# Table products and weight splits from GpSimd to VectorE, key copies to ScalarE, readout tables behind the chunk contributions

## The chip, the cores and the metric

One core of a Trainium2 chip runs the whole kernel. The metric is device microseconds of one execution, median of several runs.

## The reference

One layer for 256 latent tokens and 256 context tokens of width 1024. What the change touches lies in the first sub-layer:

```python
h  = modulate(rmsnorm(x, g1),   sh1,  sc1)      # latents
hc = modulate(rmsnorm(ctx, g1), sh1c, sc1c)     # context
proj, proj_c = h @ w_in, hc @ w_in[:, :COL_Q]   # S5 input | K | V | Q | gates
lbar = exp(lam * step); bbar = ((lbar - 1) / lam) * b
for direction in (forward, backward):           # 32 groups, 64 complex states each
    h_c = scan(lbar, u_c @ bbar)                # context, its last state starts the latents
    hs  = scan(lbar, u @ bbar, h0=h_c[end])
    y  += real(hs @ c)
q, k = rope(rmsnorm(q)), rope(rmsnorm(k))       # k of the context without rope
o = softmax(q k_all / 8) v_all
merged = gate0 * (glu(y) @ w_ssm_out) + gate1 * (o @ w_attn_out)
x_mix = x + g1 * (merged @ w_out)
```

Behind it come a second norm, a router that takes the top 4 of 32 experts, clamped SwiGLU experts of width 1024 with 12 MB of weights each, and a last norm.

## The kernel before, in words

SBUF is used as 24 pages of 1 MB (`pg(i)`), which are given out by hand. `release(p)` frees a page and issues on SP's queue the next 1 MB of a fixed list of weights: eight gate blocks of w_in, then w_glu, w_ssm_out, w_attn_out, w_out, then the experts one after the other. SP's loads stand in program order, so a load waits for its page and holds the ones behind it. The order on the other engines up to the gates is set by a scheduler that goes by its own idea of durations and of what is urgent; from `strict["on"]` on, TensorE's order is that of the program, and VectorE's, ScalarE's and GpSimd's still the scheduler's.

Products that need more than the plain pass are made from two halves of each operand: `split(src, hi, lo, eng)` rounds src into hi on ScalarE (line 62) and subtracts on `eng` (line 63). `mm3` is the three products of the halves.

The front part runs in this order:

1. Norm sums, the modulation of the first sub-layer (`mod0_mm`, `mod0_rows`), and VectorE's chain for lbar and the powers E of it, up to 47 us.
2. The input projection of the S5 branch (`u_mm`, `u_proj`). Its second half needs `wuh, wul`, split from w_in in four pieces (line 643), of which GpSimd subtracted two.
3. The S5 tables. `v_tables(qt)` for four quarters of the groups makes bbar times powers (real part VR, imaginary VI; six operations of 128x1024 in each); VI of quarters 0 and 1 lay on GpSimd. `v_transposes` turns them on TensorE. `scan_multipliers` makes the scan's constants LS (lines 521 to 529, 128x32 each). `w_tables(qt)` makes the readout tables WR, WI, c times powers, six operations of 128x1024 for each quarter, all on GpSimd (lines 608 to 613), three quarters behind `mod_tile` and the fourth behind the U copies.
4. `kv_proj`, the transposes of u into A (copies on line 704) and U (line 717).
5. The chunk contributions: `chunk_in(i)` and `chunk_T(i)` for eight pairs of group quads, copied half by VectorE (line 747), half by ScalarE (line 748); two `q_proj` lie between.
6. Rotary and norm of q and k (`rope_norm`, lines 789 to 819). A copy of each normed key block lay on GpSimd (line 822).
7. Sixteen steps u: `gate_mm(u // 2, u % 2)` multiplies the gate block whose weights `gate_split` has split (32 pieces of 128x512, subtracted on GpSimd) and asks for the next block's split; eight of the steps make `k_kernel(u)`, taps R of the S5 kernel from the W tables (last piece added on line 970); VectorE runs `scan_up` and 31 `scan_steps` (lines 855 to 858). From step 9 on attention runs beside it. R goes through DRAM (`Rd`) and comes back as Kt; `readout` uses Kt, the states and WR, WI.
8. GLU, the two branch projections, w_out, router, experts.

Of the kernel before, what the change touches and what calls it, by code (L numbers as in the profile page):

```python
# [15 lines left out]
AF = mybir.ActivationFunctionType  # L16
# [17 lines left out]
def hybrid_block(ctx: ExitStack, tc: tile.TileContext, a: dict, out: bass.AP):  # L34
    nc = tc.nc
    V, S, G, T = nc.vector, nc.scalar, nc.gpsimd, nc.tensor
# [10 lines left out]
    def renew(i, kind="f"):  # L47
        if i not in pages or epoch[i] != kind:
            pages[i], epoch[i] = pool.tile([128, PW], F32, name=f"pg{i}", tag=f"pg{i}"), kind
# [4 lines left out]
    def pg(i, o=0, n=PW):  # L54
        return pages[i][:, o:o + n]
# [5 lines left out]
    def split(src, hi, lo, eng):  # L61
        S.activation(hi.bitcast(F32R), src, AF.Copy)  # L62
        eng.tensor_sub(lo.bitcast(F32R), src, hi)  # L63
# [25 lines left out]
    def load(dst, src):  # L89
        return tc.keep_in_program_order(SP.dma_start(dst, src))  # L90
# [30 lines left out]
    def load_cols(src, c0, n, page, k0, nk):  # L121
        t = pg(page, 0, nk * n).rearrange("p (k f) -> p k f", k=nk)
        load(t, src[128 * k0:128 * (k0 + nk), c0:c0 + n].rearrange("(k p) f -> p k f", p=128))
        return t


    stream, loaded, where = [], {}, {}
# [23 lines left out]
    def release(*ps):  # L151
        for p_ in ps:
            renew(p_)
            j = state["next"]
            state["next"] = j + 1
            if j < len(stream):
                key, src = stream[j]
                k, f = src.shape[1], src.shape[2]
                t = pg(p_, 0, k * f).rearrange("p (k f) -> p k f", k=k)
                if j == len(stream) - 1:  # L160
                    for k in (0, 4):
                        load(t[:, k:k + 4], src[:, k:k + 4])
                else:
                    load(t, src)
                loaded[key], where[key] = t, p_
            elif j == len(stream):
                state["fg"] = p_
                fg_row = pg(p_, 1024, 1024)[0:1]
                load(fg_row, a["final_norm_g"][None, :])
                G.partition_broadcast(pg(p_, 0, 1024), fg_row)  # L170
# [39 lines left out]
    wu = [load_cols(w_in, 0, 512, 22, 0, 4)]  # L210
# [42 lines left out]
    def bank(hold=None):  # L253
        while True:
            i = rot["free"][rot["i"] % len(rot["free"])]
            rot["i"] += 1
            if i not in held.values():
                break
        if hold:
            held[hold] = i  # L260
        return named_bank(i)
# [288 lines left out]
    def v_part(qt, r):  # L550
        return pg(vpage[qt], 1024 * r, 1024).rearrange("p (g t k) -> p g t k", g=8, t=8)

    def v_tables(qt):
        gs = slice(8 * qt, 8 * qt + 8)
        td = pg(7, 0, 1024).rearrange("p (g t k) -> p g t k", g=8, t=8)

        def bc(r):
            return BB[:, r, gs].unsqueeze(2).to_broadcast([128, 8, 8, 16])

        def lc(r):  # L560
            return LV[:, r, :, gs].rearrange("p t g -> p g t").unsqueeze(3).to_broadcast([128, 8, 8, 16])

        VR, VI = v_part(qt, 0), v_part(qt, 1)
        V.tensor_mul(VR, bc(0), lc(0))
        V.tensor_mul(td, bc(1), lc(1))
        V.tensor_sub(VR, VR, td)
        E2 = V
        if qt < 2:
            E2, td = G, pg(20, 0, 1024).rearrange("p (g t k) -> p g t k", g=8, t=8)
        E2.tensor_mul(VI, bc(0), lc(1))  # L570
        E2.tensor_mul(td, bc(1), lc(0))
        E2.tensor_add(VI, VI, td)  # L572

    def v_transposes(qt):
        for g2 in range(4):
# [18 lines left out]
    WR, WI = [], []  # L594

    def w_tables(qt):
        gs = slice(8 * qt, 8 * qt + 8)
        td = pg(20, 1024 * (qt % 2), 1024).rearrange("p (g j k) -> p g j k", g=8, j=8)
        for r, tab in ((0, WR), (1, WI)):
            tab.append(pg((18, 19, 11, 12)[qt], 1024 * r, 1024).rearrange("p (g j k) -> p g j k", g=8, j=8))  # L600

        def cc(r):
            return CT[:, r, gs].unsqueeze(2).to_broadcast([128, 8, 8, 16])

        def lw(r):
            return LW[:, r, :, gs].rearrange("p t g -> p g t").unsqueeze(3).to_broadcast([128, 8, 8, 16])

        G.tensor_mul(WR[qt], cc(0), lw(0))
        G.tensor_mul(td, cc(1), lw(1))
        G.tensor_add(WR[qt], WR[qt], td)  # L610
        G.tensor_mul(WI[qt], cc(1), lw(0))
        G.tensor_mul(td, cc(0), lw(1))
        G.tensor_sub(WI[qt], WI[qt], td)

# [23 lines left out]
    renew(11, "r")  # L640
    wuh, wul = [pg(p_).rearrange("p (k f) -> p k f", k=4) for p_ in (12, 11)]
    for k in range(4):
        split(wu[1][:, k], wuh[:, k], wul[:, k], V if k % 2 else G)
    last = mod0_rows(1)
    del held["m", 0], held["m", 1]
    with tc.issue_after(last.ins):
# [17 lines left out]
    mod_tile()  # L664
    renew(11)
    renew(12)
    for qt in range(3):
        w_tables(qt)
    v_transposes(1)
    v_tables(3)  # L670
    v_transposes(2)
# [45 lines left out]
            V.tensor_copy(U[:, 4 * g4:4 * g4 + 4, :, h], b.rearrange("p (g q c) -> p g q c", g=4, q=4))  # L717

    mod_tile()
    w_tables(3)  # L720
    split(wq[1], wqh[1], wql[1], V)
    mod_load(16)

# [15 lines left out]
    def chunk_T(i, vo):  # L739
        b = bank()  # L740
        for j in range(2):
            for r in range(2):
                ttrans(b[:, 128 * (2 * r + j):128 * (2 * r + j) + 128],
                            vo[:, 256 * j + 128 * r:256 * j + 128 * r + 128], ident)
        for h in range(2):
            bv = b.rearrange("p (r g h c) -> p h c r g", r=2, g=4, h=2)[:, h]
            V.tensor_copy(vv[h][0:64, :, :, 4 * i:4 * i + 4], bv[0:64])
            S.activation(vv[h][64:128, :, :, 4 * i:4 * i + 4], bv[64:128, ::-1], AF.Copy)

    prev = None  # L750
    for i in range(8):
# [6 lines left out]
        if i in (2, 4):  # L758
            q_proj(i // 2 - 1)
    chunk_T(7, prev)  # L760
    release(20)
    renew(4)

    wgh, wgl_ = [pg(p_).rearrange("p (j k f) -> p j k f", j=2, k=8) for p_ in (13, 10)]

    def gate_split(i, j):
        for k in range(0, 8, GK):
            sl = slice(k, k + GK)
            split(loaded["gate", i][:, sl, 128 * j:128 * j + 128], wgh[:, j, sl], wgl_[:, j, sl], G)


    cosq, sinq = sm([128, 2, 64], "cosq"), sm([128, 2, 64], "sinq")
# [8 lines left out]
    kn = pg(5, 0, 1024).rearrange("p (t h d f) -> p t h d f", t=4, h=2, d=2)  # L781
# [31 lines left out]
    for tt in range(4):  # L813
        kvw = kv_ps[tt // 2].rearrange("p (t h f) -> p t h f", t=2, h=4)[:, tt % 2, 0:2]
        r_k = rsn[:, 16 + 2 * tt:18 + 2 * tt]
        d0 = kn[:, tt, :, 0]
        if tt < 2:
            V.tensor_mul(d0, kvw, kg_row.unsqueeze(1).to_broadcast([128, 2, 64]))
            V.tensor_mul(d0, d0, r_k.unsqueeze(2).to_broadcast([128, 2, 64]))
        else:  # L820
            rope_norm(d0, kvw, cosk[:, tt - 2], sink[:, tt - 2], r_k, 2, d0)
        G.tensor_copy(kn[:, tt, :, 1], d0)


    qs = pg(22).rearrange("p (t h r f) -> p t h r f", r=2, t=2, h=8)
# [323 lines left out]
    for u in range(16):  # L1149
# [5 lines left out]
        i = u // 2 + 1  # L1155
# [116 lines left out]
    gate, posp, ex_, mrep = [sm(sh3, n) for n in ("gate", "posp", "ex_", "mrep")]  # L1272
# [450 lines left out]
```

## Time and profile before

| what | value |
|---|---|
| median of 3 runs | 1323.57 us (1322.31 to 1325.38) |
| the profiled execution | 1321.38 us, span 1319.7 us |
| TensorE busy | 1170.8 us (89%), mean granted clock 0.966 |
| VectorE busy | 439.7 us (33%) |
| ScalarE busy | 196.5 us (15%) |
| GpSimd busy | 158.1 us (12%), 115 instructions |
| read from HBM | 459.89 MB, 350 GB/s over the span |
| chain that ended last | TensorE 49%, DMA 37%, VectorE 10% |

The shares are means over stages that differ: VectorE's and GpSimd's work lies nearly all in the first 330 us. A timeline row gives the start, the duration, the engine, the line of the program, the operation, the tiles written and read with their shapes, the count, and in brackets how long the engine stood idle before it and what ended that. A row with a count above 1 is a stretch from the first start to the last end.

### The profile page before, as it was taken

The page shows a single profiled execution, that of the slowest core. Times are in us where ns is not written, and L with a number is a line of the kernel's source. Part 1 is how long each engine was busy: PE and PEld are TensorE (multiplying, and loading weights), DVE is VectorE, ACT ScalarE, POOL GpSimd, SP SyncE. Part 2 cuts the span into 40 slices and gives each one's busy share as a digit, 9 for nine tenths or more (in the row PEclk, how much of TensorE's full clock was granted, in tenths as well). Part 3 has the DMA queues.
Part 4 walks back from the last instruction along what each step waited for, and adds up shares of the span by engine and source line. Part 5 has one row for each costly group of instructions (what it writes and reads, how often), then busy time and mean ns, then how long its engine had stood idle before and what let it go on. Part 6 is the DMA issues. An engine that isn't in the chain of part 4 may idle for free.

```text
span 1319.7 us, 16264 instructions
## 1 busy us (share of the span) xinstructions
PE 1170.8 (89%) x6711; PEld 541.5 (41%) x6712; DVE 439.7 (33%) x929; ACT 196.5 (15%) x368; POOL 158.1 (12%) x115
## 2 busy tenths in 40 slices
PE   4563998689999999999999989999898989899986
PEld 2363666578843333333332323323232323233224
DVE  5999389757331121111221111121111111111111
ACT  3231343654110000000000000000000000000001
POOL 1479563412000000000000000000000000000000
PEclk9876899889999999999999999999999999999998
DMA  9810567777989999999999999999999999999996
GB/s 277 279 33 33 191 233 240 116 219 276 352 337 416 416 417 416 416 418 417 418 418 417 418 417 416 417 416 417 417 418 417 417 417 417 417 417 415 416 392 205
DMA packets 123105, 462.57 MB, mean 351 GB/s; under 512 B 20669, under 2 KB 46953, under 8 KB 88210
## 3 DMA queue, kind: packets, MB, share of 16 engines
q1 hardware_dynamic: 122562, 460.90, 89.7%
q8 instruction: 55, 0.90, 0.3%
q0 software_dynamic: 416, 0.56, 0.1%
q14 instruction: 24, 0.20, 0.0%
q10 hardware_dynamic: 48, 0.01, 0.0%
HBM read 459.89 MB, written 1.54 MB: 350 GB/s over the span
## 4 chain that ended last, share of the span: by engine, by line
PE 49%; DMA 37%; DVE 10%; issue 2%; SPq 1%; ACT 1%; POOL 0%; DVEq 0%; ACTq 0%; POOLq 0%
PE bk L83 46%; DMA pg<-in_w_gate_up_dram 28%; DMA pg<-in_w_down_dram 7%; PE bk L86 3%; DMA pg<-Rd 1%; DVE pg L63 1%; DVE pg L858 1%; SPq L90 1%; DVE LS L528 1%; DVE LS L855 1%; DVE pg L522 0%; DVE LS L523 0%; DVE pg L848 0%; DVE pg L380 0%; DVE LS L529 0%
## 5 line engine op out<-in xcount | busy, mean ns | idle before, releaser
L83 PE MATMUL bk<-pg,pg 128*64 128x512 f32 (+6 forms) x5344 | 995.6, 476 | 65.6 <-DMA pg<-in_w_down_dram 28.3
L83 PEld LDWEIGHTS bk<-pg,pg 128*64 128x64 f32 (+3 forms) x5344 | 448.3, 154 | 552.4 <-issue 351.8
L86 PE MATMUL bk<-ident,pg 128*128 128x128 f32 x480 | 83.0, 301 | 57.3 <-DVE pg L572 21.0
L1460 DVE TENSOR_SCALAR pg<-bk 128x512 f32<-128x512 f32 x32 | 22.1, 692 | 290.7 <-PE bk L83 290.7
L1371 DVE TENSOR_TENSOR pg<-bk,shT 128x512 f32<-128x512 f32 x32 | 22.1, 692 | 266.4 <-PE bk L83 266.4
L86 PEld LDWEIGHTS bk<-ident,pg 128*128 128x128 f32 x480 | 56.6, 150 | 123.0 <-issue 48.1
L1577 POOL DMA_DIRECT2D pg<-g2d x2 | 1.3, 642 | 882.2 <-PE bk L83 882.2
L1493 DVE TENSOR_TENSOR pg<-bk,pg 128x512 f32<-128x512 f32 x30 | 20.8, 692 | 188.8 <-PE bk L83 188.8
L1472 ACT ACTIVATE pg<-bk 128x256 f32<-128x256 f32 x32 | 12.3, 383 | 395.4 <-PE bk L86 395.4
L83 PE MATMUL bk<-pg 64*128 64x512 f32 (+1 forms) x368 | 70.5, 486 | 0.0
L1477 ACT ACTIVATE pg<-bk 128x512 f32<-128x512 f32 x32 | 19.1, 596 | 257.4 <-PE bk L86 257.4
L63 POOL TENSOR_TENSOR pg<-pg,pg 128x512 fp32r<-128x512 f32 x34 | 47.5, 1412 | 43.8 <-ACT pg L62 36.8
L62 ACT ACTIVATE pg<-pg 128x512 fp32r<-128x512 f32 (+3 forms) x63 | 43.7, 721 | 56.8 <-PE bk L83 35.8
L1461 ACT ACTIVATE pg<-pg 128x512 f32<-128x512 f32 x32 | 20.1, 630 | 187.0 <-DVE pg L1460 186.9
L83 PEld LDWEIGHTS bk<-pg 64*128 64x128 f32 (+1 forms) x368 | 20.0, 162 | 50.4 <-issue 50.4
L63 DVE TENSOR_TENSOR pg<-pg,pg 128x512 fp32r<-128x512 f32 (+3 forms) x29 | 33.7, 1176 | 3.3 <-ACT pg L62 2.9
L83 PE MATMUL bk<-pg,selB 128*64 128x512 bf16 (+1 forms) x196 | 34.4, 388 | 0.0
L83 PE MATMUL bk<-pg,scond 128*32 128x256 f32 (+1 forms) x256 | 29.0, 525 | 0.0
L1462 DVE TENSOR_SCALAR pg<-bk 128x512 f32<-128x512 f32 x32 | 22.1, 692 | 5.3 <-PE bk L83 5.3
L1463 DVE TENSOR_TENSOR pg<-pg 128x512 f32<-128x512 f32 x32 | 21.8, 683 | 2.1 <-ACT pg L1461 2.0
L1464 DVE SCALAR_TENSOR_TENSOR pg<-pg 128x512 f32<-128x512 f32 x32 | 22.1, 692 | 1.1
L1468 DVE TENSOR_SCALAR pg<-iot,posp,gate 128x128 f32<-128x128 f32 x64 | 18.9, 340 | 0.0
(301 smaller groups left out, 539.1 us busy)
## 6 DMA issues: line engine op xcount, KB each, us to landing
pg<-in_w_gate_up_dram SPq DMA_DIRECT2D x256, 1024.0 KB, 20.0
pg<-in_w_down_dram SPq DMA_DIRECT2D x127, 1024.0 KB, 20.0
pg<-in_w_mod_dram SPq DMA_DIRECT2D x16, 1024.0 KB, 5.4
pg<-in_w_in_dram SPq DMA_DIRECT2D x13, 1024.0 KB, 9.0
pg<-in_w_mod_dram SPq DMA_DIRECT2D x16, 512.0 KB, 9.1
pg<-in_w_out_dram SPq DMA_DIRECT2D x4, 1024.0 KB, 11.8
pg<-Rd SPq DMA_DIRECT2D x16, 128.0 KB, 8.5
pg<-in_w_ssm_out_dram SPq DMA_DIRECT2D x2, 1024.0 KB
```

The costliest lines, as they stand in the source:

```text
L62: S.activation(hi.bitcast(F32R), src, AF.Copy)
L63: eng.tensor_sub(lo.bitcast(F32R), src, hi)
L83: pinned(T.matmul(*ar, **kw))
L86: pinned(T.transpose(*ar))
L1371: pv_(V.tensor_add(xg[p % 2][:, 4 * half:4 * half + 4], pb.rearrange("p (k m) -> p k m", k=4), shk[:, 4 * half:4 * half + 4].unsqueeze(2). ...
L1460: pv_(V.tensor_scalar(gx, pgate, 7.0, None, op0=ALU.min))
L1461: pa_(S.activation(sx, gx, AF.Sigmoid, scale=1.702))
L1462: pv_(V.tensor_scalar(ux, pup, 7.0, -7.0, op0=ALU.min, op1=ALU.max))
L1463: pv_(V.tensor_mul(gx, gx, sx))
L1464: pv_(V.scalar_tensor_tensor(ux, ux, 1.0, gx, op0=ALU.add, op1=ALU.mult))
L1477: pa_(S.activation(dst, pmx, AF.Copy))
L1493: pv_(V.tensor_mul(yx, pdn, g2h))
```

## The change

The first two V tables are made on VectorE alone. All four `w_tables` move behind the last `chunk_T` and onto VectorE, each with a scratch area of its own page instead of page 20. The two splits of w_in and all gate splits subtract on VectorE. The four key copies go to ScalarE.

```diff
--- before.py
+++ after.py
@@ -564,12 +564,9 @@
         V.tensor_mul(VR, bc(0), lc(0))
         V.tensor_mul(td, bc(1), lc(1))
         V.tensor_sub(VR, VR, td)
-        E2 = V
-        if qt < 2:
-            E2, td = G, pg(20, 0, 1024).rearrange("p (g t k) -> p g t k", g=8, t=8)
-        E2.tensor_mul(VI, bc(0), lc(1))
-        E2.tensor_mul(td, bc(1), lc(0))
-        E2.tensor_add(VI, VI, td)
+        V.tensor_mul(VI, bc(0), lc(1))
+        V.tensor_mul(td, bc(1), lc(0))
+        V.tensor_add(VI, VI, td)
 
     def v_transposes(qt):
         for g2 in range(4):
@@ -595,7 +592,7 @@
 
     def w_tables(qt):
         gs = slice(8 * qt, 8 * qt + 8)
-        td = pg(20, 1024 * (qt % 2), 1024).rearrange("p (g j k) -> p g j k", g=8, j=8)
+        td = pg((19, 11, 12, 3)[qt], 0, 1024).rearrange("p (g j k) -> p g j k", g=8, j=8)
         for r, tab in ((0, WR), (1, WI)):
             tab.append(pg((18, 19, 11, 12)[qt], 1024 * r, 1024).rearrange("p (g j k) -> p g j k", g=8, j=8))
 
@@ -605,12 +602,12 @@
         def lw(r):
             return LW[:, r, :, gs].rearrange("p t g -> p g t").unsqueeze(3).to_broadcast([128, 8, 8, 16])
 
-        G.tensor_mul(WR[qt], cc(0), lw(0))
-        G.tensor_mul(td, cc(1), lw(1))
-        G.tensor_add(WR[qt], WR[qt], td)
-        G.tensor_mul(WI[qt], cc(1), lw(0))
-        G.tensor_mul(td, cc(0), lw(1))
-        G.tensor_sub(WI[qt], WI[qt], td)
+        V.tensor_mul(WR[qt], cc(0), lw(0))
+        V.tensor_mul(td, cc(1), lw(1))
+        V.tensor_add(WR[qt], WR[qt], td)
+        V.tensor_mul(WI[qt], cc(1), lw(0))
+        V.tensor_mul(td, cc(0), lw(1))
+        V.tensor_sub(WI[qt], WI[qt], td)
 
 
 
@@ -640,7 +637,7 @@
     renew(11, "r")
     wuh, wul = [pg(p_).rearrange("p (k f) -> p k f", k=4) for p_ in (12, 11)]
     for k in range(4):
-        split(wu[1][:, k], wuh[:, k], wul[:, k], V if k % 2 else G)
+        split(wu[1][:, k], wuh[:, k], wul[:, k], V)
     last = mod0_rows(1)
     del held["m", 0], held["m", 1]
     with tc.issue_after(last.ins):
@@ -664,8 +661,6 @@
     mod_tile()
     renew(11)
     renew(12)
-    for qt in range(3):
-        w_tables(qt)
     v_transposes(1)
     v_tables(3)
     v_transposes(2)
@@ -717,7 +712,6 @@
             V.tensor_copy(U[:, 4 * g4:4 * g4 + 4, :, h], b.rearrange("p (g q c) -> p g q c", g=4, q=4))
 
     mod_tile()
-    w_tables(3)
     split(wq[1], wqh[1], wql[1], V)
     mod_load(16)
 
@@ -758,6 +752,8 @@
         if i in (2, 4):
             q_proj(i // 2 - 1)
     chunk_T(7, prev)
+    for qt in range(4):
+        w_tables(qt)
     release(20)
     renew(4)
 
@@ -766,7 +762,7 @@
     def gate_split(i, j):
         for k in range(0, 8, GK):
             sl = slice(k, k + GK)
-            split(loaded["gate", i][:, sl, 128 * j:128 * j + 128], wgh[:, j, sl], wgl_[:, j, sl], G)
+            split(loaded["gate", i][:, sl, 128 * j:128 * j + 128], wgh[:, j, sl], wgl_[:, j, sl], V)
 
 
     cosq, sinq = sm([128, 2, 64], "cosq"), sm([128, 2, 64], "sinq")
@@ -819,7 +815,7 @@
             V.tensor_mul(d0, d0, r_k.unsqueeze(2).to_broadcast([128, 2, 64]))
         else:
             rope_norm(d0, kvw, cosk[:, tt - 2], sink[:, tt - 2], r_k, 2, d0)
-        G.tensor_copy(kn[:, tt, :, 1], d0)
+        S.activation(kn[:, tt, :, 1], d0, AF.Copy)
 
 
     qs = pg(22).rearrange("p (t h r f) -> p t h r f", r=2, t=2, h=8)
```

Lines of the change are four lower from 569 on than those of before (704 is 699 or so, 855 is 851).

The order of the instructions on VectorE moves at three places. First, from the last A copies (line 704, now 699) to the first chunk copies (line 747, now 741); pg_78, pg_79 and pg_726 are pages 18, 19 and 11. Before:

```order
L704 COPY pg_727<-bk_875 128x8x64
L717 COPY pg_77<-bk_959 128x16x32
L717 COPY pg_77<-bk_965 128x16x32
L717 COPY pg_77<-bk_971 128x16x32
L717 COPY pg_77<-bk_977 128x16x32
L63 TENSOR_TENSOR pg_629<-pg_76,pg_628 128x2048
L747 COPY pg_68<-bk_1009 64x64x4
L747 COPY pg_69<-bk_1009 64x64x4
```

And in the change:

```order
L699 COPY pg_727<-bk_857 128x8x64
L605 TENSOR_TENSOR pg_78<-pg_66,pg_65 128x1024
L606 TENSOR_TENSOR pg_79<-pg_66,pg_65 128x1024
L608 TENSOR_TENSOR pg_78<-pg_66,pg_65 128x1024
L607 TENSOR_TENSOR pg_78<-pg_78,pg_79 128x1024
L606 TENSOR_TENSOR pg_726<-pg_66,pg_65 128x1024
L609 TENSOR_TENSOR pg_79<-pg_66,pg_65 128x1024
L712 COPY pg_77<-bk_941 128x16x32
```

The scheduler has drawn six operations of the W tables ahead of the U copies (line 712), although the program has them behind the chunk contributions.

Second, the end of the chunk copies. Before, the norms of k and q (lines 790 to 803) began between them:

```order
L747 COPY pg_69<-bk_1089 64x64x4
L790 TENSOR_REDUCE ssn<-pg_1188 128x4
L818 TENSOR_TENSOR pg_65<-bk_800,kg_row 128x2x64 x2
L795 TENSOR_REDUCE ssn<-pg_1188 128x8
L747 COPY pg_68<-bk_1129 64x64x4
L790 TENSOR_REDUCE ssn<-pg_1188 128x4
L802 TENSOR_TENSOR pg_65<-bk_1038,cosq 128x512
L747 COPY pg_69<-bk_1129 64x64x4
```

In the change:

```order
L741 COPY pg_68<-bk_1140 64x64x4
L609 TENSOR_TENSOR pg_63<-pg_66,pg_65 128x1024
L741 COPY pg_69<-bk_1140 64x64x4
L741 COPY pg_68<-bk_1154 64x64x4
L610 TENSOR_TENSOR pg_727<-pg_727,pg_63 128x1024
L741 COPY pg_69<-bk_1154 64x64x4
L786 TENSOR_REDUCE ssn<-pg_1188 128x4
L791 TENSOR_REDUCE ssn<-pg_1188 128x8
L786 TENSOR_REDUCE ssn<-pg_1188 128x4
L798 TENSOR_TENSOR pg_65<-bk_1014,cosq 128x512
```

The W tables now fill the places between the chunk copies, and the norms come behind the last of them.

Third, the end of the rotary stage and the first level of the scan (lines 851 to 854), in the change:

```order
L63 TENSOR_TENSOR pg_82<-pg_65,pg_82 128x8x64
L803 TENSOR_TENSOR pg_65<-pg_65,rsn 128x2x64
L63 TENSOR_TENSOR pg_308<-pg_75,pg_309 128x512 x3
L851 TENSOR_TENSOR pg_62<-pg_68,LS 128x1024
L852 TENSOR_TENSOR pg_62<-pg_68,LS 128x1024
L853 TENSOR_TENSOR pg_62<-pg_62,pg_68 128x1024
L63 TENSOR_TENSOR pg_308<-pg_80,pg_309 128x512
L854 TENSOR_TENSOR pg_68<-pg_62 128x16x64
L63 TENSOR_TENSOR pg_308<-pg_80,pg_309 128x512
L851 TENSOR_TENSOR pg_62<-pg_68,LS 128x512
```

The rows that write pg_308 are gate splits, which stood on GpSimd before; three of the first four stand behind all the rotary arithmetic, and the next ones between the levels of the scan.

## Rows read from the trace of the kernel before

**Rows 1.** Windows: stretch, length, busy PE, PEld, DVE, ACT, POOL, PEclk, DMA, GB/s.
```profile
66.00:131.00 65.00, 32.76 (x231) 29.63 (x232) 64.93 (x52) 14.20 (x21) 55.42 (x22) 0.74 0.10 33
131.00:184.00 53.00, 51.98 (x383) 35.09 (x381) 29.02 (x64) 20.99 (x42) 28.74 (x24) 0.93 0.57 191
184.00:242.00 58.00, 40.87 (x576) 31.29 (x573) 55.87 (x153) 25.54 (x50) 27.75 (x21) 0.88 0.62 205
330.00:700.00 370.00, 366.56 (x1846) 154.66 (x1847) 80.18 (x180) 29.63 (x62) 1.59 (x2) 1.00 0.99 404
700.00:1320.00 620.00, 564.55 (x2702) 196.97 (x2698) 103.75 (x207) 38.25 (x74) 2.58 (x3) 0.99 1.00 404
```

**Rows 2.** Timeline of SP's queue, the experts' first loads.
```profile
301.44 1.45 SPq L90 DMA_DIRECT2D pg<-in_w_gate_up_dram  x2
```

**Rows 3.** Timeline of VectorE, 68 to 85 us.
```profile
68.78 1.21 DVE L565 TENSOR_TENSOR pg<-pg,pg 128x1024 f32<-128x1024 f32 x1
69.91 1.21 DVE L564 TENSOR_TENSOR pg<-pg,pg 128x1024 f32<-128x1024 f32 x1
...
73.49 0.17 DVE L528 COPY LS<-LS 128x32 f32<-128x32 f32 x1
...
76.24 2.06 DVE L523 TENSOR_TENSOR LS<-pg 128x32 f32<-128x32 f32 x1
...
82.39 2.02 DVE L528 COPY LS<-LS 128x32 f32<-128x32 f32 x1
```

**Rows 4.** Timeline of GpSimd, its first W product.
```profile
75.58 2.68 POOL L608 TENSOR_TENSOR pg<-pg,pg 128x1024 f32<-128x1024 f32 x1 [10.73 <-ACT pg L591]
```

**Rows 5.** Timeline of VectorE, 29 to 147 us.
```profile
29.10 0.42 DVE L367 COPY pg<-bk 128x256 f32<-128x256 f32 x1
...
30.86 1.38 DVE L380 TENSOR_SCALAR pg<-pg,gsc,shc 128x256 f32<-128x256 f32 x4
...
50.81 5.25 DVE L63 TENSOR_TENSOR pg<-pg,pg 128x512 fp32r<-128x512 f32 x2 [0.19 <-PE bk L83]
...
65.23 1.21 DVE L564 TENSOR_TENSOR pg<-pg,pg 128x1024 f32<-128x1024 f32 x1
66.37 2.48 DVE L63 TENSOR_TENSOR pg<-pg,pg 128x512 fp32r<-128x512 f32 x4
...
133.59 1.87 DVE L704 COPY pg<-bk 128x512 f32<-128x512 f32 x3
144.64 2.48 DVE L717 COPY pg<-bk 128x512 f32<-128x512 f32 x4 [9.18 <-PE bk L86]
```

**Rows 6.** Timeline of ScalarE, a 128x256 instruction.
```profile
168.83 0.38 ACT L789 ACTIVATE pg<-bk 128x256 f32<-128x256 f32 x1
```

**Rows 7.** Timeline of VectorE, 168 to 242 us.
```profile
168.01 0.48 DVE L818 TENSOR_TENSOR pg<-bk,kg_row 128x128 f32<-128x128 f32 x2
...
176.64 0.41 DVE L747 COPY pg<-bk 64x256 f32<-64x256 f32 x1
...
185.67 1.30 DVE L856 TENSOR_TENSOR pg<-pg,LS 128x1024 f32<-128x1024 f32 x1
...
202.31 0.23 DVE L858 TENSOR_TENSOR LS<-pg 128x64 f32<-128x64 f32 x1
...
203.93 1.20 DVE L858 TENSOR_TENSOR pg<-LS 128x64 f32<-128x64 f32 x1
...
241.39 0.21 DVE L970 TENSOR_TENSOR pg<-bk,Dm 128x64 f32<-128x64 f32 x1
```

**Rows 8.** Timeline of TensorE, 240 to 250 us.
```profile
240.24 1.11 PE L86 MATMUL bk<-ident,pg 128*128 128x128 f32 x4 [10.58 <-ACT pg L929]
241.01 5.16 PE L83 MATMUL bk<-pg,pg 128*128 128x256 f32 x26
...
246.36 3.58 PE L83 MATMUL bk<-pg,pg 128*128 128x256 f32 x26
```

**Rows 9.** The chain of waits, the way of R through DRAM.
```profile
241.68 4.41 DMA Rd<-pg
...
268.45 8.02 PE bk L83 x118
```

## The prediction, made before the result was known

> **What bounds the kernel now.** I read the windows first, then VectorE's and GpSimd's timelines side by side, then TensorE's and the chain of waits. The windows show three regimes [rows 1]. From 66 to 131 us VectorE is busy 64.9 of 65 us and GpSimd 55.4, while TensorE has work for half of it and the DMA engines move 33 GB/s. From 131 to 184 TensorE is full (52.0 of 53 us) and VectorE idles 24.0. From 184 to 242 VectorE is full again (55.9 of 58). From 700 to the end the weights set the pace: DMA share 1.00 at 404 GB/s. The experts' first load is issued at 301.44 us [rows 2], and their loads wait for pages that the front part frees. So a microsecond saved ahead of the experts is a microsecond at the end, provided the page releases move with it.
>
> What the reader is to see in VectorE's timeline is that its busy time is not work. A product of 128x1024 starts 1.13 us after the one in front (68.78, 69.91), a 128x32 copy takes 0.17 us at 73.49, before GpSimd starts, and the same line 2.02 us at 82.39, when it runs; the operation at 76.24 ends at 78.30, and GpSimd's product ends at 78.26 [rows 3, 4]. So while GpSimd works on SBUF, VectorE's next such operation stands until GpSimd's instruction ends; the two take turns. Every GpSimd product that is moved therefore costs VectorE its own 1.13 us and gives back a turn of about 2 us.
>
> **The change, part by part.** Moved to VectorE: 6 products and sums of the first two V tables, 24 of the W tables (128x1024 each), 2 weight splits of w_in and 32 gate splits (128x512). At 1.13 us, and 0.60 us for 128x512 (four in 2.48 us [rows 5]), that is 33.9 + 20.4 = 54.3 us of own time. Moved to ScalarE: four copies of 128x128, under 0.38 us each by the 128x256 row [rows 6], 1.5 us on an engine that is busy 21 of 53 us there [rows 1]; cost 0; if that cover were gone, 1.5 us. No queue gains a DMA. SP's gate loads lose their wait on GpSimd and take one on VectorE.
>
> (1) *50.8 to 65.2 us.* Both versions start the splits of w_in when TensorE has let go of page 11. Before, two splits took 5.25 us and the first V product came at 65.23 [rows 5]. Now VectorE does four splits, 2.4 us, then the rows of mod0, 1.8 us in the first half where GpSimd stood still (29.10 to 30.86), then four modulations, 1.38 us [rows 5]: the product comes at 56.4. **-8.8.**
>
> (2) *From there to the last A copy.* Before: 65.23 to 135.46, the end of the last three copies [rows 5]; 70.2 us. Now, as the order shows, 24 table operations of 1.13 (27.1), four splits of 0.60 (2.4), two of 128x2048 at four times 0.60 (4.8), four A copies at 0.62 (2.5), and 28 operations on the scan multipliers at 0.10 to 0.18 apart (4.0): 40.8 us. **-29.4.** TensorE's 32.8 us of work in that stretch [rows 1] fits, just.
>
> (3) *The chunk contributions.* Six W operations (6.8 us) now lie between A and U copies, where VectorE waited 9.18 us for TensorE [rows 5]. The other 18 (20.3 us) lie between the chunk copies: with U copies 2.5, one split 2.4 and 16 copies of 0.41 [rows 7] that makes 32 us, against the 32.4 us that TensorE's pace took from the first U copy to the last chunk copy's end (144.64 to 177.05 [rows 5, 7]). This cover is nearly used up. The copies free the PSUM banks that TensorE writes next, so a copy behind four or five products stands 5 us. Between 0 and 8; I take **+3**, since two projections of q give TensorE other work there.
>
> (4) *The rotary stage.* Before, its first 9 us ran between the last chunk copies, so that only 8.6 us lay behind the last of them (177.05 to 185.67 [rows 7]). Now, by the order, it starts after the last one: 16 operations of 128x512 (9.6, four gate splits among them), 12 of 128x128 at 0.20 (a pair takes 0.48 [rows 7]; 2.4), two reductions and 12 tiny ones (1.8), and the first product of the scan, which was already done before (1.1): 14.9 us. **+6.3.**
>
> (5) *The scan up, 185.67 to 202.5.* Before 16.9 us with GpSimd's turns in it [rows 7]. Now three operations of 128x1024 (3.4), four each of 512, 256, 128 and 64 columns (2.4, 1.4, 0.8, 0.6), five of 128x512 for q and k (3.0), four gate splits (2.4) and some 1 us where one waits for the result of the last: 15. **-1.9.**
>
> (6) *Scan steps until the last piece of the tap table R is there, 202.5 to 241.6 [rows 7].* Before 39.1 us, of which some nine operations of 1.2 us whose own time is 0.23 (203.93 against 202.31) give 9 back. Now 11 splits (6.6) come in, and two steps of four such operations (1.6) fall behind R: 39.1 - 9 + 6.6 - 1.6 = 35.1. **-4.0.**
>
> (7) *New waits.* The first gate matmuls waited for GpSimd's splits, done early; now their splits stand inside and behind the rotary arithmetic, so TensorE idles some 12 us between the last chunk transpose and the gates, and each later gate block waits for splits that stand behind scan steps on VectorE. The first wait is inside (4) as long as VectorE is the later one: in 184 to 242 TensorE had 40.9 us of work and VectorE 55.9 [rows 1], and in the sums above VectorE keeps 50. For the lockstep I take **+3**, between 0 (VectorE later everywhere) and 14 (a gap like the 10.58 us one [rows 8] once more, and some).
>
> On the clock: behind that 10.58 us gap, 26 matmuls of the gate took 5.16 us against 3.58 us later [rows 8]. The Trainium skill (TensorE: Matmul & The Clock Gate, Part 1) says that an array that stood idle runs at half clock until it has been busy again. By that rule the new 12 us gap costs 1.6 us more and the sum would be 1.6 smaller; The trace agrees in kind: the mean granted clock is 0.74 of full speed from 66 to 131 us and 1.00 where TensorE is hardly ever out of work [rows 1]. I take 0 for it, because VectorE, not TensorE, is the later engine there.
>
> (8) *R to the end.* R goes to DRAM at 241.68 and comes back as Kt before TensorE's 268.45 [rows 9]: 27 us of transfers that no part touches. From 330 to 700 TensorE is busy 366.6 of 370 us [rows 1]. Cost 0; GpSimd's last splits here go to a VectorE with a third of its time free. Bounds -2 to +3.
>
> Sum: -8.8 - 29.4 + 3 + 6.3 - 1.9 - 4.0 + 3 + 0 = **-32**. The profiled execution took 1321.38 us for a span of 1319.7, which is 2.2 under the median of the runs: 1289 on its own scale, **1291** on that of the median.
>
> **Rivals.**
> *A, lockstep.* GpSimd was a second worker for the gate splits; on one in-order engine, eight gate blocks each wait 1 to 2 us for a split behind the scan, on top of the first gap. Against: VectorE, not TensorE, is full in that stage already. +14 for (7) instead of 3, +8 for (3) instead of 3: gain 16 us, **1307**.
> *B, more than summed.* Chunk copies never hold TensorE, no lockstep, TensorE's clock stays up: 3 + 3 + 4 back (the 4 from TensorE's matmuls at the faster clock in 66 to 131): **1281**.
> *C, slower.* The 2 us rows are VectorE's own (say, an operation that waits for its predecessor's result), not turns of GpSimd. Then nothing is given back: 8 us in 47 to 131, 27.1 us of W tables beyond the idle 24.0 us of the chunk stage 3, sixteen splits beyond the 2.1 us left in 184 to 242 about 8: **1343**. It decides if the small operations keep 2 us without GpSimd. Against: line 528 with the same predecessor took 0.17 us while GpSimd stood still [rows 3], and the long ones end with GpSimd's [rows 4].
> *D, no change.* The front gets faster and the weights arrive no earlier. Then 1323. Against: in 66 to 131 us the DMA engines moved 33 GB/s [rows 1], so they wait for pages.
>
> **How the numbers follow.** Forecast 0.66, A 0.15, B 0.12, C 0.04, D 0.03. The forecast alone spans 1283 to 1300. The range has to take in most of A and B: low 1280, high 1307. A measurement of this kernel tells about 0.2% (2.6 us) from no change. Faster: all of forecast, A and B, 0.93; same 0.03; slower 0.04.
>
> **What would show it.** Right: the scan multiplier operations at 0.2 us each; last A copy near 97 us; last chunk copy near 142; R complete near 209; the first experts' load issued 30 us earlier than at 301; from 700 on the same pace. (3) is wrong if TensorE shows gaps behind chunk copies of over 5 us; (7) if gate matmuls wait for VectorE's line 63 by more than 5 us in sum beyond the first gap. The prediction as a whole is wrong if VectorE is still full from 47 to 131 us.

## The result, and the profile after

The changed kernel takes **1284.14 us** (median of 4 runs, 1282.1 to 1286.1) against 1323.14 us of the kernel before on the same chip. The ratio is 0.9703, with a 95% interval of 0.9682 to 0.9723: 39 us faster, where the prediction said 32 (1291, range 1280 to 1307). The profiled execution took 1282.10 us for a span of 1280.4; the one before had a span of 1319.7.

I read the windows first. The columns are those of [rows 1].

```profile
66.00:131.00 65.00, 59.70 (x417) 44.79 (x416) 61.37 (x86) 26.31 (x44) 9.68 (x11) 0.95 0.37 131
131.00:184.00 53.00, 40.43 (x530) 29.25 (x533) 51.44 (x151) 22.61 (x48) 2.89 (x4) 0.87 0.68 228
184.00:242.00 58.00, 47.17 (x589) 40.70 (x588) 40.40 (x130) 32.82 (x59) 2.27 (x4) 0.91 0.78 152
700.00:1280.00 580.00, 527.51 (x2520) 183.52 (x2516) 97.14 (x194) 36.24 (x70) 2.58 (x3) 0.99 0.99 403
```

From 66 to 131 us VectorE is still nearly full (61.4 of 65 us), but it now gets 86 instructions done instead of 52, and TensorE is busy 59.7 us instead of 32.8. GpSimd, busy 55.4 us there before, has 9.7 left. The last row is as before (403 against 404 GB/s): the experts keep their pace, and what is won ahead of them stays won.

VectorE's timeline of the changed kernel answers to [rows 3, 5, 7]. Its lines 605 to 610 are lines 608 to 613 of the kernel before, 699 is 704, 712 is 717 and 741 is 747.

```profile
49.35 2.49 DVE L63 TENSOR_TENSOR pg<-pg,pg 128x512 fp32r<-128x512 f32 x4 [1.94 <-PE bk L83]
...
54.99 1.22 DVE L564 TENSOR_TENSOR pg<-pg,pg 128x1024 f32<-128x1024 f32 x1
...
77.33 0.17 DVE L528 COPY LS<-LS 128x32 f32<-128x32 f32 x1
77.42 0.17 DVE L521 TENSOR_TENSOR pg<-LS 128x32 f32<-128x32 f32 x1
...
94.46 1.27 DVE L699 COPY pg<-bk 128x512 f32<-128x512 f32 x2
95.66 1.21 DVE L605 TENSOR_TENSOR pg<-pg,pg 128x1024 f32<-128x1024 f32 x1
...
104.56 2.48 DVE L712 COPY pg<-bk 128x512 f32<-128x512 f32 x4 [2.02 <-PE bk L86]
...
137.56 0.41 DVE L741 COPY pg<-bk 64x256 f32<-64x256 f32 x1
...
152.78 1.22 DVE L852 TENSOR_TENSOR pg<-pg,LS 128x1024 f32<-128x1024 f32 x1
...
166.60 0.21 DVE L854 TENSOR_TENSOR LS<-pg 128x64 f32<-128x64 f32 x1
```

Line 528, a 128x32 copy that took 2.02 us at 82.39 before [rows 3], takes 0.17. Four splits of w_in take 2.49 us where two took 5.25 [rows 5]. The W products (from 95.66) stand in the wait for TensorE, which falls from 9.18 to 2.02 us.

TensorE's timeline, with the waits in brackets, answers to [rows 8, 9]:

```profile
146.27 2.93 PE L83 MATMUL bk<-pg,pg 128*128 128x256 f32 x12 [10.21 <-DVE pg L63]
150.57 2.50 PE L83 MATMUL bk<-pg,pg 128*128 128x256 f32 x10 [1.37 <-DVE pg L63]
...
198.71 1.12 PE L86 MATMUL bk<-ident,pg 128*128 128x128 f32 x4 [2.71 <-ACT pg L925]
...
227.60 8.73 PE L83 MATMUL bk<-pg,pg 128*32 128x128 f32 x118 [6.12 <-DMA pg<-Rd]
```

And SP's queue answers to [rows 2, 9]:

```profile
201.20 3.64 SPq L90 DMA_DIRECT2D Rd<-pg  x8
...
261.30 1.45 SPq L90 DMA_DIRECT2D pg<-in_w_gate_up_dram  x2
```

The new gap of 10.2 us ahead of the gates is there (12 had been forecast), the 10.58 us one further on has shrunk to 2.71, and the experts' first load is issued at 261.30 instead of 301.44.

From these rows the span splits into stages. Each row is the time from the event above it; the last column is the prediction's term.

| stage, up to | before | after | change | predicted |
|---|---|---|---|---|
| first split of w_in | 50.81 | 49.35 | -1.5 | 0 |
| first V product | 14.42 | 5.64 | -8.8 | (1) -8.8 |
| end of the last A copy | 70.23 | 40.74 | -29.5 | (2) -29.4 |
| end of the last chunk copy | 41.59 | 42.24 | +0.6 | (3) +3 |
| second product of the scan | 8.62 | 14.81 | +6.2 | (4) +6.3 |
| top of the scan (line 854 to LS) | 16.64 | 13.82 | -2.8 | (5) -1.9 |
| write of R | 39.37 | 34.60 | -4.8 | (6) -4.0 |
| readout | 26.77 | 26.40 | -0.4 | (8) 0 |
| experts' first load | 32.99 | 33.70 | +0.7 | (8) 0 |
| end of the span | 1018.26 | 1019.10 | +0.8 | (8) 0 |
| sum | 1319.7 | 1280.4 | -39.3 | -32, with (7) +3 |

The first row is not put down to the change: before, VectorE was also ready first and waited 0.19 us for TensorE at this split [rows 5], as it waits 1.94 now. In the twelve profiles below that split starts anywhere from 49.2 to 53.9 us.

### The profile page after: what moved, and what is told of

It reads as the page before. It is cut to its first block, busy times and chain, and to the rows that moved or that the text cites. A ratio compares the mean times of both kernels' runs of the same rounds, so it can differ in the third digit from the quotient of the medians.

```text
span 1280.4 us, 16234 instructions
## 1 busy us (share of the span) xinstructions
PE 1168.5 (91%) x6711; PEld 539.0 (42%) x6712; DVE 424.1 (33%) x993; ACT 197.2 (15%) x372; POOL 37.4 (3%) x47
## 4 chain that ended last, share of the span: by engine, by line
PE 57%; DMA 31%; DVE 7%; issue 2%; SPq 1%; ACT 0%; POOL 0%; DVEq 0%; POOLq 0%; ACTq 0%
PE bk L83 54%; DMA pg<-in_w_gate_up_dram 28%; PE bk L86 3%; DMA pg<-in_w_down_dram 2%; DMA pg<-Rd 1%; DVE pg L63 1%; SPq L90 1%; DVE pg L565 0%; DVE pg L568 0%; DVE pg L566 0%; DVE pg L564 0%; DVE pg L569 0%; DVE pg L567 0%; DVE pg L854 0%; DVE pg L844 0%
## 5 line engine op out<-in xcount | busy, mean ns | idle before, releaser
L86 PE MATMUL bk<-ident,pg 128*128 128x128 f32 x480 | 80.1, 292 | 16.1 <-DVE pg L367 4.2
L63 DVE TENSOR_TENSOR pg<-pg,pg 128x512 fp32r<-128x512 f32 (+3 forms) x63 | 49.9, 803 | 16.4 <-ACT pg L62 14.3
L62 ACT ACTIVATE pg<-pg 128x512 fp32r<-128x512 f32 (+3 forms) x63 | 44.0, 721 | 53.0 <-PE bk L83 38.9
L1357 DVE TENSOR_SCALAR pg<-iot,posp,rs 128x64 f32<-128x64 f32 x64 | 15.7, 307 | 0.1
```

What stands on the lines that cost most here:

```text
L86: pinned(T.transpose(*ar))
```

## Experiments: one part at a time

Two theories are tested. **Turns**: while GpSimd works on SBUF, VectorE's next operation of the kinds in [rows 3] stands, so GpSimd's work costs VectorE more than it relieves it. **Place, or VectorE's own**: the rows of 2 us have nothing to do with GpSimd, and what counts is only where the W tables stand. Beside them is **lockstep**: gate splits on VectorE hold TensorE up.

Four kernels ran beside each other on one chip, with 5 rounds, the changed kernel itself among them.

> The changed kernel as it is, for comparison on one chip with the three variants beside it. Every theory: 1284 us, within 3.

Measured: 1285.34 us (1284.21 to 1286.27), ratio to before 0.9713 [0.9700, 0.9726]. "The changed kernel" below is this run.

**Gate splits back on GpSimd.**

```
-            split(loaded["gate", i][:, sl, 128 * j:128 * j + 128], wgh[:, j, sl], wgl_[:, j, sl], V)
+            split(loaded["gate", i][:, sl, 128 * j:128 * j + 128], wgh[:, j, sl], wgl_[:, j, sl], G)
```

> One part undone: the 32 gate splits (128x512) go back from VectorE to GpSimd, all else as in the changed kernel. Theory (turns: while GpSimd works on SBUF, VectorE's next operation on SBUF stands): in the scan and its steps the 128x64 operations of line 851 to 854 show rows of 1.2 us again, where they take 0.22 now; the stretch from the scan's second product to the write of R, 48.4 us now, goes back toward the 56.0 us of before, +5 to +8; the rotary stage loses four splits of 0.60 us, -2.4, and TensorE's 10.2 us gap before the gates shrinks, since GpSimd can split the first gate block behind the last chunk copies. In sum +4 us (0 to +8). Rival (lockstep: splits on VectorE hold TensorE up, and a second engine is worth more than the turns cost): -3 to -8 us.

Measured: 1295.03 us, 0.9785 [0.9772, 0.9799]: 9.7 us slower, somewhat beyond the range. GpSimd's timeline, then VectorE's, of this kernel:

```profile
171.74 1.38 POOL L63 TENSOR_TENSOR pg<-pg,pg 128x512 fp32r<-128x512 f32 x1 [2.61 <-ACT pg L62]
...
177.90 2.58 POOL L63 TENSOR_TENSOR pg<-pg,pg 128x512 fp32r<-128x512 f32 x2 [3.30 <-ACT pg L62]
```

```profile
125.54 2.31 DVE L609 TENSOR_TENSOR pg<-pg,pg 128x1024 f32<-128x1024 f32 x1
...
171.99 1.21 DVE L854 TENSOR_TENSOR pg<-LS 128x64 f32<-128x64 f32 x1
...
173.76 0.22 DVE L854 TENSOR_TENSOR pg<-LS 128x64 f32<-128x64 f32 x1
...
178.03 1.30 DVE L853 TENSOR_TENSOR LS<-LS,pg 128x64 f32<-128x64 f32 x1
```

A scan operation that meets a gate split on GpSimd takes 1.2 to 1.3 us and ends with it (173.20 against 173.12); the same line without one takes 0.22. From the top of the scan (170.37) to the write of R (209.87) it takes 39.5 us, where the changed kernel takes 34.6 and the kernel before 39.4 [rows 7, 9]: this part of the gain is the gate splits' alone. Lockstep, as something that costs more than the turns, falls. Beyond the expectation were the chunk stage, 2.9 us longer (GpSimd's first gate splits take turns with VectorE's W products there, as the row at 125.54 shows with 2.31 us for an operation that takes 1.21 alone; I had counted this as free), and R's way to the readout, 1.4 us. The rotary stage, which was to lose 2.4 us, lost 0.4.

**Key copies back on GpSimd.**

```
-        S.activation(kn[:, tt, :, 1], d0, AF.Copy)
+        G.tensor_copy(kn[:, tt, :, 1], d0)
```

> One part undone: the four 128x128 copies of the normed keys go back from ScalarE to GpSimd. Theory (turns): each copy, 1.0 us on GpSimd before, can hold one VectorE operation in the rotary stage or the scan for up to 1 us: +1 us (0 to +3). Rival (ScalarE's queue pays for these copies, or nothing does): 0, or up to 1 us faster.

Measured: 1284.95 us, 0.9708 [0.9692, 0.9724]: no difference that can be told. If this part of the change is worth anything here, it is less than these runs can tell.

**First gate splits ahead of the rotary stage.** The three lines that split and release the first gate block are moved from in front of the scan to in front of the rotary tables.

> The changed kernel with the splits of the first gate block written ahead of the rotary stage instead of behind it; work and engines the same. If VectorE alone sets the end of this stretch: 0 (within 2 us), since the order of the same work on a full engine does not change its sum. If TensorE, once it has its gate splits, is the bound until the tap table (it shows gaps of 1.4 and 1.0 us only from 146 to 196 us): its gap of 10.2 us before the gates falls to some 4 us and the tap table's transfer, issued at 201.2 us now, starts 4 to 6 us earlier: -5 us.

Measured: 1287.42 us, 0.9728 [0.9715, 0.9742]: 2.1 us slower, so at best no gain. TensorE's timeline of this kernel:

```profile
139.90 2.89 PE L83 MATMUL bk<-pg,pg 128*128 128x256 f32 x22 [2.56 <-DVE pg L63]
147.38 1.94 PE L83 MATMUL bk<-pg,scond 128*32 128x512 f32 x8 [4.58 <-DVE pg L817]
...
163.99 1.12 PE L86 MATMUL bk<-ident,pg 128*128 128x128 f32 x4 [6.08 <-DVE pg L902]
```

The gates start 7 us earlier, and TensorE then waits 4.6 and 6.1 us for VectorE's lines 817 and 902. R is written at 204.3 us, not earlier than the changed kernel's 202.0. The gap of 10.2 us has shrunk to 2.56, and two others have come behind it. So it is not on the path: VectorE sets the end of this stretch, as term (7) assumed.

The clock is to be seen here too. In the changed kernel the 22 gate matmuls behind the gap took 2.93 + 2.50 = 5.43 us, and the mean granted clock from 146.2 to 153.1 us was 0.50 of full speed, the lower of its two levels (1.2 GHz); here, behind a wait of 2.56 us, they took 2.89 us at 1.00 (2.4 GHz, 139.9 to 142.8 us). The Trainium skill (TensorE: Matmul & The Clock Gate, Part 1) has an array that stood idle at half clock, and the trace agrees. But in this kernel the lower level comes behind the next wait: 0.50 from 147.3 to 150.0 us, where the eight matmuls at 147.38 take 1.94 us, against 1.07 for eight of the same kind at 154.52. The slow stretch was moved and not removed, so no run shows what the clock by itself is worth.

Four more kernels ran on one chip, with 3 rounds; before took 1324.15 us there, as beside the first four (1324.19), so they are compared through it.

**V tables and w_in splits alone**, in the kernel before:

```
-        E2 = V
-        if qt < 2:
-            E2, td = G, pg(20, 0, 1024).rearrange("p (g t k) -> p g t k", g=8, t=8)
-        E2.tensor_mul(VI, bc(0), lc(1))
+        V.tensor_mul(VI, bc(0), lc(1))
...
-        split(wu[1][:, k], wuh[:, k], wul[:, k], V if k % 2 else G)
+        split(wu[1][:, k], wuh[:, k], wul[:, k], V)
```

> The kernel before with one part of the change alone: the first two V tables and the weight splits of w_in go to VectorE; W tables, gate splits and key copies stay on GpSimd. Theory (turns): from the first of these splits to the first V product 5.6 us in place of 14.4 (-8.8); the scan multipliers, which stood behind GpSimd's W products, can run before GpSimd has its C tables at 75 us, at 0.1 to 0.2 us each; behind that the W products still take turns with V tables, splits and h splits. Last A copy near 120 us (135.5 before, 95.7 with the whole change), and about -15 us at the end: 1308 (1300 to 1315). Rival (the small operations' 2 us are VectorE's own): they keep 2 us, and the time is 1323 or more.

Measured: 1322.15 us, 0.9981 [0.9970, 0.9992]: 2 us, a clear miss of the 15. GpSimd's first W product and VectorE's timeline of this kernel:

```profile
65.89 3.64 POOL L605 TENSOR_TENSOR pg<-pg,pg 128x1024 f32<-128x1024 f32 x1 [50.41 <-ACT pg L588]
```

```profile
56.04 1.22 DVE L564 TENSOR_TENSOR pg<-pg,pg 128x1024 f32<-128x1024 f32 x1
...
70.71 2.03 DVE L528 COPY LS<-LS 128x32 f32<-128x32 f32 x1
...
132.50 1.27 DVE L701 COPY pg<-bk 128x512 f32<-128x512 f32 x2
```

The first V product is early by the 8.8 us. But the C tables came early too, so GpSimd began its W products at 65.89 instead of 75.58 [rows 4] and met the scan multipliers all the same. GpSimd still made 19 W products ahead of the last A copy, as in the kernel before, and the six products taken over cost VectorE 6 x 1.13 = 6.8 us: from the first V product to the last A copy 77.7 us, 7.5 more than before. What was won ahead was paid back behind.

**W tables alone**: the lines of `w_tables` and their place as in the changed kernel, all else as before.

> The kernel before with the other large part alone: the W tables go to VectorE, behind the chunk contributions; V tables, the splits of w_in, gate splits and key copies stay on GpSimd. Theory (turns): the 14.4 us before the first V product stay (+8.8 against the whole change), GpSimd's six V products take six turns of about 2 us less 6 times 1.13 us (+5), the gate splits' turns come back (+4): 1284 + 18 = 1302 (1295 to 1310). Rival (the gain comes from the W tables alone): 1287 or less.

Measured: 1300.29 us, 0.9823 [0.9807, 0.9840]: 23.9 us faster than before, near the 1302 expected. Added to the kernel before, the V tables with the splits of w_in give 2.0 and the W tables 23.9; taken out of the changed kernel, the gate splits cost 9.7 and the key copies -0.4. Together that is 35.2 of the 38.9 us, but the two kinds of number are not the same: the 2.9 us that the gate splits cost in the chunk stage come from meeting W products on VectorE, which the kernel before does not have there. No run shows the gate splits alone in the kernel before, so which parts make up the other 3.7 us stays open. What the last two runs do show is that the W tables carry most of the gain, and that the V tables bring next to nothing while GpSimd still makes the W tables.

**W tables on VectorE in their old place.** (Their scratch area is page 20 again.)

```
+    for qt in range(3):
+        w_tables(qt)
     v_transposes(1)
...
     mod_tile()
+    w_tables(3)
...
     chunk_T(7, prev)
-    for qt in range(4):
-        w_tables(qt)
```

> The changed kernel with the W tables on VectorE, but in the place where they were before: three quarters ahead of the second V transposes, the last behind the U copies. It tells the engine from the place. Theory: 18 operations of 1.13 us come in ahead of the A copies, where VectorE is full, +20; the chunk stage is set by TensorE either way and gives back at most 1 us: last A copy near 116 us, +19 us (15 to 22), 1303. Rival (the move off GpSimd is all that counts, the place hides nothing): within 3 us of 1284.

Measured: 1297.27 us, 0.9799 [0.9780, 0.9818]: 12 us slower than the changed kernel, not 19. The 20 us are there: from the first V product to the last A copy it takes 61.2 us against 40.7. But the time from the last chunk copy to the scan shrinks from 14.8 to 6.2 us. VectorE's timeline:

```profile
134.06 1.20 DVE L610 TENSOR_TENSOR pg<-pg,pg 128x1024 f32<-128x1024 f32 x1
...
149.82 0.67 DVE L799 TENSOR_TENSOR pg<-bk,cosq 128x512 f32<-128x512 f32 x1
...
156.77 0.41 DVE L744 COPY pg<-bk 64x256 f32<-64x256 f32 x1
```

With the W tables done at 135 us, the rotary stage starts between the chunk copies again, as in the kernel before. So the cover behind the chunk contributions is one and the same for both: the change gave it to the W tables and pushed the rotary stage out. I had booked that in term (4) and forgot it in this expectation.

**W tables on GpSimd, in the new place.** In `w_tables` the six operations go back to G; the call stays behind the chunk contributions.

> The changed kernel with the W tables in their new place behind the chunk contributions, but on GpSimd. Theory (turns): the part up to the last A copy stays as in the changed kernel (95.7 us); behind it GpSimd needs 24 products of 2 to 3 us, 50 to 75 us, so until 147 to 172 us; the chunk copies read PSUM and are not held, but the rotary stage and the scan take turns, and the tap kernels, which TensorE reached at 154.5 us, wait for the last table: +12 us (4 to 25). Rival (only the place counts: VectorE has enough room behind, whoever does the tables): within 3 us of 1284.

Measured: 1307.57 us, 0.9879 [0.9857, 0.9902], 22 us slower than the changed kernel. It isn't the experiment that was meant: nothing held GpSimd back, its first W product started at 68.13 us, and the last A copy ended at 125.3 us instead of 96.5. It had 14 of its 24 products ahead of the A copies. Against the run in front of it, with 18 of 24 there on VectorE, it is 10 us slower: at nearly the same place GpSimd is the dearer engine. The run was repeated with a hold (w_late_g2, below).

## Experiments: the cost by itself, and a better version

Two kernels with 3 rounds and two with 5 on one chip (before: 1324.66 us). The changed kernel stood on another chip: the differences to it are those of the medians, and by the ratios each of the four comes out 1 to 2.3 us better.

**Eight products that nobody needs.**

```
+        gx = G.tensor_copy(sm([128, 4], "gx"), v_part(0, 0)[:, 0, 0, 0:4])
+        for n_ in range(8):
+          with tc.issue_after(gx.ins):
+            G.tensor_mul(pg(20, 1024 * (n_ % 2), 1024), BB.rearrange("p r g k -> p (r g k)"), BB.rearrange("p r g k -> p (r g k)"))
```

> The disputed cost by itself: the changed kernel, and on GpSimd, behind the first V table, eight extra 128x1024 products of one table with itself, written to a free page that nobody reads. VectorE's own work, its order and its inputs stay as they are. Theory (turns): each extra product makes one VectorE operation on SBUF stand for about 2 us, in 56 to 95 us where VectorE is full: the last A copy comes 16 us later (12 to 20), and so does the end: about 1300. Rival (the rows of 2 us were VectorE's own, or came with the W tables): last A copy and end within 2 us of the changed kernel.

Measured: 1298.89 us, 0.9808 [0.9793, 0.9823]: 13.6 us slower than the changed kernel. GpSimd's timeline, then VectorE's:

```profile
67.47 19.48 POOL L649 TENSOR_TENSOR pg<-pg 128x1024 f32<-128x1024 f32 x8
```

```profile
68.68 1.89 DVE L528 COPY LS<-LS 128x32 f32<-128x32 f32 x1
70.49 0.17 DVE L529 TENSOR_SCALAR LS<-LS 128x32 f32<-128x32 f32 x1
...
71.71 1.92 DVE L521 TENSOR_TENSOR pg<-LS 128x32 f32<-128x32 f32 x1
73.55 1.93 DVE L522 TENSOR_TENSOR pg<-LS 128x32 f32<-128x32 f32 x1
...
95.05 0.18 DVE L521 TENSOR_TENSOR pg<-LS 128x32 f32<-128x32 f32 x1
...
109.25 1.27 DVE L703 COPY pg<-bk 128x512 f32<-128x512 f32 x2
```

No result of GpSimd is used, VectorE's work is the same, and still rows of 1.9 us are back, eight of them for eight products, and gone when GpSimd is done (95.05). From the first V product to the last A copy it takes 54.7 us against 40.7: 13.9 us for eight products, 1.74 each. This is the price of a turn, and it shows the theory without any of the change's own edits; the rival, that these rows are VectorE's own, falls.

**W tables on GpSimd, held.**

```
+    gx = G.tensor_copy(sm([128, 4], "gx"), U[:, 7, 0, 1, 0:4])
+    with tc.issue_after(gx.ins):
+        for qt in range(4):
+            w_tables(qt)
```

> The W tables on GpSimd as in w_late_g, but now held until the U copies are there (a 128x4 copy of the last of them on GpSimd, behind which the products are queued; in w_late_g nothing held them and they started at 68 us). Theory (turns): last A copy near 96 us as in the changed kernel; then 24 products of 2.0 to 2.4 us, 108 to 160 us or later; VectorE's chunk copies from PSUM are not held, and part of the rotary stage fits between them again (8.5 us, as in w_early_v), but what it does on SBUF takes turns, and the tap kernels, at 154.5 us now, wait for the last table: +6 us (-2 to +15). Rival (only the place counts, not the engine): within 2 us of 1285.

Measured: 1308.52 us, 0.9872 [0.9857, 0.9887]: 23 us slower than the changed kernel, well outside the range. GpSimd's, VectorE's and TensorE's timelines:

```profile
123.02 2.03 POOL L608 TENSOR_TENSOR pg<-pg,pg 128x1024 f32<-128x1024 f32 x1
...
132.69 2.46 POOL L608 TENSOR_TENSOR pg<-pg,pg 128x1024 f32<-128x1024 f32 x1
...
159.25 2.01 POOL L609 TENSOR_TENSOR pg<-pg,pg 128x1024 f32<-128x1024 f32 x1
```

```profile
123.35 0.42 DVE L741 COPY pg<-bk 64x256 f32<-64x256 f32 x1 [1.32 <-PE bk L86]
...
133.93 0.67 DVE L793 TENSOR_REDUCE ssn<-pg 128x8 f32<-128x512 f32 x1
...
161.29 0.69 DVE L800 TENSOR_TENSOR pg<-bk,cosq 128x512 f32<-128x512 f32 x1 [26.04 <-POOL pg L609]
```

```profile
162.77 1.97 PE L83 MATMUL bk<-pg,pg 128*64 128x256 f32 x8 [28.79 <-ACT pg L742]
```

It is mostly not turns that cost this. The rotary stage writes q into columns 1024 on of page 5, where LW lies, which the W tables read; so its first product waited 26 us for the last reader of LW, the chunk copies queued behind it on VectorE, and TensorE stood 28.8 us. I had priced the engine and not the page. So this run doesn't separate turns from place. Ballast8 and gsplit_back show the turns, and w_early_v the place.

**R earlier.**

```
-        if P_K <= u < 8 + P_K:
-            k_kernel(u - P_K)
-        if u == 7 + P_K:
+        if 2 <= u < 6:
+            k_kernel(2 * u - 4)
+            k_kernel(2 * u - 3)
+        if u == 5:
...
+        if u == 6:
+            kernel_in(0)
```

> An attempt at a better version: the changed kernel with two tap kernels per step in steps 2 to 5 in place of one per step in 0 to 7, the write of R behind step 5, and the first half of its return (page 6) behind step 6, the second half (page 9, which the scan holds) behind step 9 as before. If the way of R through DRAM is what the readout waits for (a gap of 6 to 7 us on TensorE at 221 to 228 us, ended by the transfer), that gap goes: -6 us (-3 to -8). If TensorE's and VectorE's own work up to the readout sets the time, or the earlier transfers hold up the gate weights on SP's queue: 0, or slower by up to 5 us.

Measured: 1283.91 us, 0.9685 [0.9672, 0.9699]: 1.4 us faster than the changed kernel by the medians, 3.7 by the ratios, not 6. SP's queue, VectorE's and TensorE's timelines:

```profile
193.22 3.85 SPq L90 DMA_DIRECT2D Rd<-pg  x8
197.25 3.75 SPq L90 DMA_DIRECT2D pg<-Rd  x8
...
218.93 3.76 SPq L90 DMA_DIRECT2D pg<-Rd  x8
```

```profile
216.89 2.01 DVE L881 COPY pg<-pg 64x992 f32<-64x992 f32 x2
```

```profile
229.50 7.93 PE L83 MATMUL bk<-pg,pg 128*32 128x128 f32 x118 [7.73 <-DMA pg<-Rd]
```

R is out 9 us earlier and half of it is called back at 197, but the second half goes to page 9, which the scan's copies on VectorE let go at 218.90. The gap in front of the readout stays at 7.7 us. R's way and the scan end nearly together; taking one away leaves the other.

**And some of VectorE's work to ScalarE.**

```
-        V.tensor_scalar(pb, pb, ssum[:, c_i:c_i + 1], None, op0=ALU.mult)
+        S.activation(pb, pb, AF.Copy, scale=ssum[:, c_i:c_i + 1])
```

and ScalarE copies both halves of each query transpose.

> As r_early, and two kinds of VectorE operations (the 128x512 copy of half of each query transpose, 0.68 us, and the scaling of the probabilities, 0.48 us) go to ScalarE, which is busy for 51 of the 100 us from 142 to 242. If VectorE sets the end of this stretch, its 2 x 0.60 + 7 x 0.40 us ahead of the readout come off: 2 to 4 us faster than r_early. If ScalarE's chain of exponentials is what the transposes wait for: 0 to 3 us slower than r_early.

Measured: 1279.51 us, 0.9660 [0.9647, 0.9674]: 4.4 us faster than r_early and 5.8 faster than the changed kernel. VectorE, whose scan copies hold page 9, was the one to relieve: the second half of R is now called back at 213.08. No run has this relief without the earlier R. It is the fastest version here, faster than both kernels; its interval lies wholly below the changed kernel's [0.9700, 0.9726].

## Why the prediction was right, and where it was off

The sign, the mechanism and the place were right, and 1284 lies in the range; the sum was 7 us too small. Of the signs that it named, the short operations of the scan multipliers (0.17 us at 77.33, up to 0.49 where GpSimd still makes the rotary tables), the last A copy (95.7 us, forecast near 97), the last chunk copy (138.0, near 142), R (written at 201.2, near 209) and the experts' first load (40 us earlier, 30 forecast) came as said or earlier. One sign was badly set: the prediction was to be wrong if VectorE is still full from 47 to 131 us, and it is busy there for 77.6 of 84 us, 82.8 before. By the prediction's own terms (2) and (3) it had to be nearly full; what changed is that it gets 113 instructions done there instead of 69. The stated span of the forecast, 1283 to 1300, also does not follow: with (3), (7) and (8) all at their upper bounds the sum gives 1310. Point by point, by the table of stages:

- **(1) and (2)** came out to 0.1 us: -8.8 and -29.5. Nearly the whole net gain stands here; the later terms almost cancel. They rest on counting turns: VectorE's own 1.13 us per product against the rows of 2 us; ballast8 shows such a turn at 1.74 us.
- **(3)** was mis-sized: +0.6 instead of +3. TensorE shows no gap behind the chunk copies in the changed kernel. The six W operations ahead of the U copies and the two projections of q left enough room for copies that come late.
- **(4)** was right at +6.2, and w_early_v shows why it had to be paid: the rotary stage and the W tables want the same idle time.
- **(5) and (6)** were right in kind and 1.7 us short. gsplit_back gives the steps back (34.6 to 39.5 us).
- **(7)** was the wrong term. The gap of 10 us ahead of the gates is there, but no stage of the table has room for a +3; the one further wait for line 63 ahead of the readout is 1.4 us (150.57), under the 5 named. gs_first shows that even the big gap costs nothing that can be told, since VectorE is later. By the prediction's own terms the gate splits were worth about 0.5 us (2.4 in (4) and 3 in (7) against 1.9 and 4.0); gsplit_back measures 9.7, of which 2.9 belong to the chunk stage of the changed kernel.
- **(8)** cost +1.1 over three rows. The 27 us of R's way stayed, at 26.4.
- 1.5 us of the profiled difference arose ahead of the change, and is scatter of single executions.

Of the rivals, A (lockstep) is refuted by gsplit_back, C by ballast8, D by the first load at 261.30. B was right in two of its three grounds: the chunk copies did not hold TensorE and there was no lockstep. Its third, that TensorE gains from the faster clock (0.74 to 0.95 in 66 to 131 us), is not visible, since (2) came out by VectorE's sum alone.

## What to carry to other kernels

When a helper engine and VectorE both work on SBUF, price the helper by what VectorE stands, not by the helper's own time: find a short operation of one line with and without the helper running. When work is moved into idle time, ask who used that idle time before, and which page the moved work holds until its last read. An idle gap on an engine is worth a move only if that engine, and not another, ends the stretch: cutting TensorE's 10 us gap to 2.6 gained nothing, and relieving VectorE by a few operations of 0.4 to 0.6 us, with R already early, gained 4.4.

## What the runs showed of the hardware

- A turn spares some operations. In w_late_g2, while GpSimd worked without a pause, VectorE's chunk copies from PSUM took 0.42 us (123.35) and a reduction over 512 columns 0.67 (133.93), as without GpSimd, while copies and products with their inputs in SBUF stood for about 1.9 us in ballast8. The Trainium skill (SBUF — State Buffer, SBUF: two separate sides, with its part Who interferes with whom) gives the two engines a shared pair of ports that one of them holds for its whole instruction, and leaves out VectorE's operations with at most one input in SBUF unless they run in a two-port mode. These rows agree, if the 128x32 copy at 68.68 in ballast8, which has one input in SBUF and stood, ran in such a mode; no row shows the mode.
- The turn goes both ways, and the two do not always alternate. GpSimd's product of line 771 took 9.05 us at 57.86 in the changed kernel, where VectorE ran seven products one behind the other (58.53 to 66.5 us) before it ended, and 0.45 us in w_late_g2 (line 773 there, at 57.89), where VectorE ran short operations. In gsplit_back, where four gate splits met four W products, they took one each in turn (the row at 125.54). What decides between the two, no run shows.

```profile
57.86 9.05 POOL L771 TENSOR_TENSOR cosq<-pg,qg_row 128x128 f32<-128x128 f32 x1 [42.90 <-DMA pg<-in_rope_dram]
```

- A 128x1024 product of two SBUF inputs takes GpSimd 2.01 us with VectorE idle (159.25 in w_late_g2) and VectorE 1.13 from start to start.
